# SwiGLU's upward products from the fifth block on as seven half-depth products, in a decoder trunk of fp32 weights split in two

## Chip, cores and metric

The kernel runs on one core of a Trainium2 chip. The metric is the device time of one execution in microseconds (us).

## The reference

One inference step of a trunk of two layers, on 512 columns of a prompt and 64 of eight samples. Each layer is an FFN, a mixer (retention, a Conformer convolution, a gated short convolution) and a second FFN; shift, scale and gate of each come from a conditioning vector by one more product ("modulation", `w_ada`).

```python
def swiglu(h, w1, w3, w2):
    return (jax.nn.silu(h @ w1) * (h @ w3)) @ w2
...
    ada = jax.nn.silu(c) @ w['w_ada'] + w['b_ada']
...
    h = modulate(rms_norm(x, w['g_ffn1']), sh1, sc1)
    x = x + 0.5 * gt1 * swiglu(h, w['w1_a'], w['w3_a'], w['w2_a'])
    h = modulate(rms_norm(x, w['g_mix']), sh2, sc2)
    mo, S_new, conf_new, sc_new = mixer(h, state_ret[l], state_conf[l], state_sconv[l], pos0, w)
    x = x + gt2 * mo
    h = modulate(rms_norm(x, w['g_ffn2']), sh3, sc3)
    x = x + 0.5 * gt3 * swiglu(h, w['w1_b'], w['w3_b'], w['w2_b'])
```

`h` has 1024 rows, w1 and w3 2816 columns each, w2 goes back to 1024. All is fp32.

## The kernel before

**Tiles.** Features lie on the partitions, the 576 columns in two halves of 288. A weight block of 128 outputs has 8 depth tiles of 128. Each fp32 number is split into a high part (a cast to fp32r) and a low part (the rest), and each product of 128x128 with 128x288 is three matmuls, hi.hi, hi.lo and lo.hi (`three`, L210 to L212). The hidden state `h` is held split in `hh` and `hl`.

**FFN.** Four FFNs run, called ffn0a, ffn0b, ffn1a and ffn1b here (layer, first or second). Each has 22 blocks f of w1 and w3. A block pair is one step: for each half, w1's and w3's product over all 8 depth tiles, then `post` (silu on ACT, L611; product on DVE, L612; split by ACT, L225, and DVE, L226). After the blocks of each entry of `GROUPS` come the 8 down products with w2 for these blocks. The last group's last four run in `end`, which lays the statistics of the next norm over its products: `stats` after one block of the first of them, `spread` (which needs a chain of small DVE operations, L317 to L343) after another of the second.

**Weights.** `pump` brings weights in along the list of keys of all steps. A 512 KB DMA on SP's queue fills one of RAW = 3 raw buffers (L142), ACT casts its high part (L161), DVE subtracts the low part (L121), and the raw buffer is free when DVE is done. Up to WB = 5 split weights are held. SP issues its DMAs in the order of the program, and an issue that must wait holds up those behind it.

**Modulation units.** While layer 0 runs, the modulation of everything later is computed in units (`ada_unit`): two tiles of 256 KB (L135) and four matmuls of 256 columns (L277). Two units stand behind nearly each block pair of ffn0a and ffn0b, one or two behind a down product. Up to ADA = 12 tiles are loaded ahead. Layer 1 has none.

**POOL** works in the mixers and in the norms, and adds the gated result of the sample columns to `xs` in the down products (L590).

## Time and profile before

| what | us |
| --- | --- |
| median of 3 runs | 3136.75 (3132.89 to 3136.88) |
| the profiled execution | 3134.75 |
| its span, first to last instruction | 3133.0 |
| TensorE busy in it | 3091.1 |

The profile is that of one execution; the span is what its rows cover, and 1.75 us lie around it. The mean granted TensorE clock was 0.996 of full speed (2.4 GHz).

### The profile page before, as it was taken

How to read it: one execution, taken by the hardware profiler on the slowest of the kernel's cores; microseconds unless marked ns; L12 is line 12 of the kernel's file. 1: busy time of each engine (PE TensorE's matmuls, PEld its weight loads, DVE VectorE, ACT ScalarE, POOL GpSimd, SP SyncE). 2: the span in 40 equal slices, each digit the busy share in tenths (PEclk: the TensorE clock that was granted, in tenths of full speed). 3: DMA queues.
4: the chain of work that ended last, by engine and by line, in shares of the span. 5: the costliest groups of instructions: out<-in, count | busy, mean ns of one | idle time of the engine just before them, and what ended most of it. 6: DMA issues, size and time to landing. Idle time of an engine off the chain costs nothing.

```text
span 3133.0 us, 55305 instructions
## 1 busy us (share of the span) xinstructions
PE 3091.1 (99%) x23412; PEld 2969.0 (95%) x23412; DVE 1535.0 (49%) x2840; ACT 873.4 (28%) x1468; POOL 405.7 (13%) x526
## 2 busy tenths in 40 slices
PE   7999999999999999999999999999999999999998
PEld 5999999899999999999999999988999999999998
DVE  5333336355995563323363333453669854533334
ACT  4222223222233342222232222332222333422221
POOL 1000004123113020000020000042221220200000
PEclk9999999999999999999999999999999999999999
DMA  7544423334322334636322222233352222222221
GB/s 277 167 155 149 148 94 125 100 85 116 89 77 80 115 122 147 207 129 214 113 82 75 88 88 81 88 117 112 84 120 84 81 95 95 78 85 81 81 83 56
DMA packets 142680, 349.67 MB, mean 112 GB/s; under 512 B 32400, under 2 KB 36752, under 8 KB 142432
## 3 DMA queue, kind: packets, MB, share of 16 engines
q1 hardware_dynamic: 135776, 329.35, 33.1%
q0 software_dynamic: 5504, 15.61, 1.9%
q8 instruction: 183, 3.00, 0.4%
q10 hardware_dynamic: 1152, 1.18, 0.1%
q14 instruction: 65, 0.53, 0.1%
HBM read 328.90 MB, written 12.45 MB: 109 GB/s over the span
## 4 chain that ended last, share of the span: by engine, by line
PE 92%; DVE 3%; POOL 1%; ACT 1%; DMA 1%; issue 1%; SPq 0%; ACTq 0%; DVEq 0%; POOLq 0%
PE pl L210 28%; PE pl L211 27%; PE pl L212 27%; PE pm L277 2%; PE pl L765 1%; PE pl L767 1%; PE pl L766 1%; PE pm L1164 1%; PE pm L1166 1%; DVE lo L121 1%; DMA ada<-in_ada 1%; DVE hl L383 1%; DVE t L393 0%; ACT hi L161 0%; DMA x<-in_x 0%
## 5 line engine op out<-in xcount | busy, mean ns | idle before, releaser
L211 PE MATMUL pl<-hl,hi 128*128 128x288 f32 x4576 | 1350.2, 295 | 11.0 <-POOL hl L421 9.6
L210 PE MATMUL pl<-hh,hi 128*128 128x288 f32 x4576 | 1360.3, 297 | 0.3 <-ACT hh L419 0.2
L212 PE MATMUL pl<-hh,lo 128*128 128x288 f32 x4576 | 1349.8, 295 | 0.0
L210 PEld LDWEIGHTS pl<-hh,hi 128*128 128x128 f32 x4576 | 860.2, 188 | 21.5 <-DVE t L612 10.7
L211 PEld LDWEIGHTS pl<-hl,hi 128*128 128x128 f32 x4576 | 860.2, 188 | 13.5 <-POOL hl L421 10.8
L212 PEld LDWEIGHTS pl<-hh,lo 128*128 128x128 f32 x4576 | 859.9, 188 | 0.0
L121 DVE TENSOR_TENSOR lo<-raw,hi 128x1024 fp32r<-128x1024 f32 (+1 forms) x446 | 551.8, 1239 | 520.0 <-ACT hi L161 519.7
L161 ACT CAST hi<-raw 128x1024 fp32r<-128x1024 f32 (+1 forms) x446 | 459.0, 1032 | 836.7 <-PE pl L211 635.6
L210 PE MATMUL pl<-ghi,hi 128*128 128x288 f32 x1408 | 419.9, 298 | 0.0
L212 PE MATMUL pl<-ghi,lo 128*128 128x288 f32 x1408 | 415.2, 295 | 0.0
L211 PE MATMUL pl<-glo,hi 128*128 128x288 f32 x1408 | 415.1, 295 | 0.0
L590 POOL TENSOR_TENSOR xs<-xs,t 128x64 f32<-128x64 f32 x112 | 41.1, 367 | 1833.8 <-DVE t L587 1833.6
L612 DVE TENSOR_TENSOR t<-t,pl 128x288 f32<-128x288 f32 x176 | 79.9, 454 | 404.1 <-PE pl L212 389.6
L210 PEld LDWEIGHTS pl<-ghi,hi 128*128 128x128 f32 x1408 | 264.4, 188 | 13.6 <-issue 11.5
L211 PEld LDWEIGHTS pl<-glo,hi 128*128 128x128 f32 x1408 | 264.5, 188 | 0.0
L212 PEld LDWEIGHTS pl<-ghi,lo 128*128 128x128 f32 x1408 | 264.4, 188 | 0.0
L210 PE MATMUL pl<-s,hi 128*128 128x288 f32 x768 | 227.8, 297 | 0.1
L211 PE MATMUL pl<-s,hi 128*128 128x288 f32 x768 | 226.6, 295 | 1.1 <-DVE s L226 1.1
L212 PE MATMUL pl<-s,lo 128*128 128x288 f32 x768 | 226.7, 295 | 0.0
L957 DVE SCALAR_TENSOR_TENSOR cv<-up,vec,cv 128x512 f32<-128x512 f32 x240 | 209.3, 872 | 5.4
L225 ACT CAST ghi<-t 128x288 fp32r<-128x288 f32 x176 | 76.1, 432 | 480.4 <-DVE t L612 480.4
L210 PEld LDWEIGHTS pl<-s,hi 128*128 128x128 f32 x768 | 144.3, 188 | 3.7 <-ACT t L867 2.1
(197 smaller groups left out, 2686.5 us busy)
## 6 DMA issues: line engine op xcount, KB each, us to landing
ada<-in_ada SPq DMA_DIRECT2D x288, 256.0 KB, 4.6
raw<-in_win SPq DMA_DIRECT2D x120, 512.0 KB, 3.6
raw<-in_w1a SPq DMA_DIRECT2D x44, 512.0 KB, 3.6
raw<-in_w3a SPq DMA_DIRECT2D x44, 512.0 KB, 3.6
raw<-in_w1b SPq DMA_DIRECT2D x44, 512.0 KB, 3.6
raw<-in_w3b SPq DMA_DIRECT2D x44, 512.0 KB, 3.6
raw<-in_w2a SPq DMA_DIRECT2D x32, 512.0 KB, 3.5
raw<-in_w2b SPq DMA_DIRECT2D x32, 512.0 KB, 3.5
```

The lines of the kernel that those rows point to most:

```text
L121: self.nc.vector.tensor_sub(lo, t, hi.bitcast(F32))
L161: nc.scalar.copy(hi[:, :m], t[:, c])
L210: mm(ps[:, :HB], hi[:, c], x[0][:, t], start=first, stop=False)
L211: mm(ps[:, :HB], hi[:, c], x[1][:, t], start=False, stop=False)
L212: mm(ps[:, :HB], lo[:, c], x[0][:, t], start=False, stop=last)
L225: nc.scalar.copy(hi, src)
L277: nc.tensor.matmul(self.ps_ada[32 * j:32 * j + 32, :], self.cs[:, k], w, start=(k == 0), stop=(k == 7))
L383: nc.vector.scalar_tensor_tensor(self.hl[:, k, c], t, s, hi.bitcast(F32), ALU.add, ALU.subtract)
L590: nc.gpsimd.tensor_add(xs, xs, t[:].rearrange("p b t -> p (b t)"))
L612: nc.vector.tensor_mul(s, s, ps[1][:, :HB])
L765: mm(ps, xh, wh, start=(k == 0), stop=False)
L957: nc.vector.scalar_tensor_tensor(cv[:, :S], up[:, k:k + S], w[:, k:k + 1], cv[:, :S], ALU.mult, ALU.add)
```

## The change

Blocks 0 to 3 of each FFN stay as they were, but block 3 runs its second half first. From block 4 on, two blocks f and f+1 ("a duo") are taken together, first w1 of both, then w3 of both. With the depth cut into a first and a second half of four tiles and the columns into halves, this is a 2x2 by 2x2 product of blocks, and `seven` computes it with seven products of half depth instead of eight: 7 x 4 x 3 matmuls on weights X, Y, Z (two tiles of 512 columns each, Y and Z made in place of the raws b and a) and S, which are sums of the raws' halves.

- `sums` makes these sums with four POOL additions of 128x512 and queues the casts as jobs. A pump in a seven does at most one job (`once`). A seven's casts are X, Y and Z of 1024 columns and S of 512, in place of two of 1024 for the two blocks.
- `forms` makes the matching sums of `h` (T2, T4, T5) in blocks 0 to 3; `last_forms` overwrites the second half of `hh` and `hl` in the middle of block 3. Until then `hold` keeps the first `sums` back.
- The results are put together behind the products: an ACT copy (s1), three DVE additions (u, v, u), and in `up1` and `up3` further ones; up3 multiplies three of its four results on POOL, and its splits run one post later.
- Two modulation units ("mids") stand inside each seven of ffn0a and ffn0b, between the third product and the fourth, as long as units are left, and one behind it. One stands behind each down product. Once the start is over only ADA_LATER = 4 tiles are loaded ahead, and pump takes their keys out of the list.
- `GROUPS` has four entries, the last with 6 blocks in place of 8; RAW goes from 3 to 4, SLOTS from 38 to 37, TEMPS from 12 to 10.
- The layernorm of the Conformer branch takes its mean with ones and a factor of -1/512 in the DVE operation, and the tile `one512` goes.

```diff
-GROUPS = ((0, 6), (6, 8), (14, 8))
+GROUPS = ((0, 6), (6, 6), (12, 4), (16, 6))
...
-RAW, WB, AHEAD, ADA = 3, 5, 4, 12
+RAW, WB, AHEAD, ADA, ADA_LATER = 4, 5, 4, 12, 4
...
-SLOTS, TEMPS = 38, 12
+SLOTS, TEMPS = 37, 10
...
-    def pump(self, later=False):
+    def load_ada(self, key):
+        self.split[key] = self.slot([128, 512], what="ada")
+        self.nc.sync.dma_start(self.split[key], self.source(key)[0])
+        self.whole += 1
+    def pump(self, later=False, cast=True):
         nc = self.nc
+        once = not cast
+        self.calls += 1
+        while self.gone and self.gone[0] <= self.calls:
+            self.gone.popleft()
+            self.whole -= 1
...
+            if self.quota > 8:
+                while self.n_dma < len(self.keys) and self.keys[self.n_dma][0] == "ada":
+                    self.adas.append(self.n_dma)
+                    self.n_dma += 1
+                if self.adas and self.whole < ADA_LATER and self.adas[0] <= self.cur + 2 * ADA:
+                    self.load_ada(self.keys[self.adas.popleft()])
+                    went = True
...
+            if self.jobs:
+                if not once and self.live + self.jobs[0][0] <= WB:
+                    self.jobs.popleft()[1]()
+                    if not later:
+                        self.rest()
+                    went = once = True
+            elif self.raw and self.quota and not (once and cast) and self.order[self.raw[0][0]] <= self.order[self.cur] + AHEAD:
                 key = self.keys[self.raw[0][0]]
                 spare = key in self.spare
-                if spare or self.live < WB:
+                if key in self.duo:
+                    if len(self.raw) > 1 and not self.hold:
+                        self.sums(key, self.raw.popleft()[1], self.raw.popleft()[1])
+                        went = True
...
+    def halves(self, key, t, n=1024):
+        w = [self.wp.tile([128, 1024], F32R, tag=x, bufs=WB, name=self.name(x)) for x in ("hi", "lo")]
+        self.live += 1
+        self.nc.scalar.copy(w[0][:, :n], t[:, :n])
+        self.late.append((w[1][:, :n], t[:, :n], w[0][:, :n]))
+        self.split[key] = w
...
+    def sums(self, key, a, b):
+        add = self.nc.gpsimd.tensor_add
+        s = self.wp.tile([128, 512], F32, tag="s1", bufs=1, name=self.name("s1"))
+        add(s, b[:, :512], b[:, 512:])
+        add(b[:, :512], b[:, :512], a[:, :512])
...
+        def z():
+            self.rest()
+            add(a[:, :512], a[:, :512], s)
+            add(a[:, 512:], a[:, 512:], a[:, :512])
+        def zh():
+            self.halves((*key, "Z"), a)
+            self.held -= 1
+        def yh():
+            self.halves((*key, "Y"), b)
+            self.held -= 1
+        self.jobs.extend(((1, lambda: self.halves((*key, "X"), a)), (0, z),
+                          (1, lambda: self.halves((*key, "S"), s, 512)), (1, yh), (1, zh)))
...
-            self.whole -= 1
+            if self.quota > 8:
+                self.gone.append(self.calls + 1)
+            else:
+                self.whole -= 1
...
+            nc.vector.tensor_sub(za[:, a], za[:, a], za[:, b])
+            nc.vector.tensor_sub(za[:, b], za[:, b], zb[:, b])
+            nc.vector.tensor_add(zb[:, b], zb[:, b], za[:, a])
+            nc.vector.tensor_sub(zb[:, a], zb[:, b], zb[:, a])
+            t5 = self.slot([128, NT], F32R, "t5")
...
+        self.T[7] = [(self.hh[:, i, HB:NT], self.hl[:, i, HB:]) for i in range(4)]
...
+    def last_forms(self):
+        for i, z in enumerate(self.zs):
+            hi, lo = self.T[7][i]
+            self.nc.scalar.copy(hi, z[:, HB:])
+            self.nc.vector.tensor_sub(lo, z[:, HB:], hi.bitcast(F32))
...
+        def product(ps, which, at, xs, first, last):
+            hi, lo = self.part(key, which)
+            for i, x in enumerate(xs):
+                c = slice(512 * at + 128 * i, 512 * at + 128 * i + 128)
+                k = dict(skip_group_check=True)
+                mm(ps, hi[:, c], x[0], start=first and i == 0, stop=False, **k)
+                mm(ps, hi[:, c], x[1], start=False, stop=False, **k)
+                mm(ps, lo[:, c], x[0], start=False, stop=last and i == 3, **k)
...
+        def more():
+            self.rest()
+            for fn in self.after:
+                fn()
+            self.after = []
+            self.pump(True)
+        p, q = bank(), bank()
+        product(p, "X", 0, quarter(0, 0), True, True)
+        s1 = self.temp([128, HB])
+        nc.scalar.copy(s1, p)
+        more()
+        product(q, "Y", 0, self.T[7], True, True)
+        u, v = self.temp([128, HB]), s1
+        nc.vector.tensor_add(u, s1, q)
+        more()
+        product(p, "X", 1, quarter(1, 0), False, True)
+        free("X")
+        post(0, 0, p)
+        more()
+        self.ada_done()
+        for m in mids:
+            self.ada_unit(*m)
+        product(q, "Z", 0, self.T[2], False, True)
+        nc.vector.tensor_sub(v, s1, q)
+        nc.vector.tensor_sub(u, u, q)
+        more()
+        r = bank()
+        product(r, "S", 0, self.T[5], True, True)
+        free("S")
+        post(1, 1, v, r)
+        more()
+        t = bank()
+        product(t, "Y", 1, self.T[4], True, True)
+        free("Y")
+        post(1, 0, v, t)
+        more()
+        product(r, "Z", 1, quarter(1, 1), False, True)
+        free("Z")
+        post(0, 1, u, r)
+        self.rest()
+        self.pump(True, False)
...
-            ps = self.run(w, xs, 1, 0, {0: 4, 1: 6}.get(i), {0: stats, 1: spread}.get(i))
+            ps = self.run(w, xs, 1, 0, {0: len(xs) // 2, 1: 3 * len(xs) // 4}.get(i), {0: stats, 1: spread}.get(i))
...
+            halves = (1, 0) if f == 3 else (0, 1)
...
+                if half > halves[1]:
+                    self.drain()
+                    self.last_forms()
+                    self.hold = False
+                    self.pump()
...
+            def up1(i, j, a, b=None):
+                t = self.temp([128, HB])
+                if b is None:
+                    nc.scalar.activation(t, a, AF.Silu)
+                else:
+                    if i == 0:
+                        nc.vector.tensor_add(t, a, b)
+                    else:
+                        nc.vector.scalar_tensor_tensor(t, a, -1.0, b, ALU.mult, ALU.subtract)
+                    nc.scalar.activation(t, t, AF.Silu)
+                acts[i, j] = t
+            def up3(i, j, a, b=None):
+                s = acts.pop((i, j))
+                if b is None:
+                    nc.vector.tensor_mul(s, s, a)
+                else:
+                    t = self.temp([128, HB])
+                    if i == 0:
+                        nc.vector.tensor_add(t, a, b)
+                    else:
+                        nc.vector.scalar_tensor_tensor(t, a, -1.0, b, ALU.mult, ALU.subtract)
+                    nc.gpsimd.tensor_mul(s, s, t)
+                c = slice(j * HB, (j + 1) * HB)
+                hi, lo = (x[:, c] for x in g[f + i])
+                def halves():
+                    nc.scalar.copy(hi, s)
+                    nc.vector.tensor_sub(lo, s, hi.bitcast(F32))
+                waiting.append(halves)
...
-                elif f > 1 or first:
-                    self.steps.append((pairs[f], lambda f=f: pair_step(pairs[f])))
-                    add_fill(0 if first and f == 5 else 2)
-            final = gi == 2
+                elif f > 3:
+                    for up in range(2 - f % 2 * 2):
+                        ks = [pairs[f][up], pairs[f + 1][up]]
+                        mids = [fill.popleft() for _ in range(min(2, len(fill)))]
+                        ks += [("ada", *u, i) for u in mids for i in range(2)]
+                        self.steps.append((ks, lambda f=f, up=up, mids=mids: duo_step(f, up, mids)))
+                        add_fill(2 if nfill > 72 else 1)
...
-                add_fill(2 if nfill > 60 else 1)
+                add_fill(1)
```

Three places show how instructions move. The first is SP's queue in ffn0b. Before, around blocks 12 and 13, the raws of one pair are followed by four modulation tiles (the word behind L142 or L135 is the tile; in brackets stands what the issue waits for, a DMA's completion or an engine):

```order
L142 DMA raw1752_12164<-in_w1b 128x1024 [waits DMAHW4_49,DVE_49]
L142 DMA raw1762_12242<-in_w3b 128x1024 [waits DMAHW5_49,DMAHW6_49,DVE_49,Activation_49]
L135 DMA ada1763_12244<-in_ada 128x512 [waits DMASW1_49,PE_49]
L135 DMA ada1764_12246<-in_ada 128x512 [waits DMAHW7_49,PE_49]
L135 DMA ada1765_12248<-in_ada 128x512 [waits DMAHW0_49,PE_49]
L135 DMA ada1766_12250<-in_ada 128x512 [waits DMAHW1_49,PE_49]
L142 DMA raw1794_12423<-in_w1b 128x1024 [waits DMAHW2_49,DVE_49]
L142 DMA raw1801_12489<-in_w3b 128x1024 [waits DMAHW4_49,DMAHW3_49,DVE_49]
```

After, at the last duos that have units, each seven queues the raws a and b of a later seven and then six tiles, or fewer. The tiles ada2660 and ada2661 are those of the second mid unit of the seven that follows, and raw2652 ahead of them waits for DVE's lo2651, the Z of that same seven, written at the turn to it; ada2690 and ada2691, for the second mid unit of the seven after, stand behind raw2678, which waits for lo2677, its Z:

```order
L167 DMA raw2647_16553<-in_w3b 128x1024 [waits DMAHW2_49,DVE_49]
L167 DMA raw2652_16575<-in_w3b 128x1024 [waits DMAHW3_49,DVE_49]
L136 DMA ada2660_16622<-in_ada 128x512 [waits DMAHW4_49,PE_49]
L136 DMA ada2661_16624<-in_ada 128x512 [waits DMAHW5_49,PE_49]
L136 DMA ada2665_16660<-in_ada 128x512 [waits DMAHW6_49,PE_49]
L136 DMA ada2666_16662<-in_ada 128x512 [waits DMAHW7_49,PE_49]
L136 DMA ada2667_16683<-in_ada 128x512 [waits DMAHW0_49,PE_49]
L136 DMA ada2668_16685<-in_ada 128x512 [waits DMAHW1_49,PE_49]
L167 DMA raw2673_16708<-in_w1b 128x1024 [waits DMAHW2_49,DVE_49,Activation_49]
L167 DMA raw2678_16732<-in_w1b 128x1024 [waits DVE_49,DMAHW3_49,Activation_49,Pool_49]
L136 DMA ada2690_16787<-in_ada 128x512 [waits DMAHW4_49,PE_49]
L136 DMA ada2691_16789<-in_ada 128x512 [waits DMAHW5_49,PE_49]
```

The loads have moved from up to six units ahead of their use to a place behind the second raw that is queued at the turn into the seven that uses them.

The second place is DVE at the end of the up3 seven of that duo and the start of the next up1 seven. L874 is the last addition after the seventh product (in pl2669), L883 a low part of a gated value, lo2672 and lo2677 are Y and Z of the next seven, lo2682 X of the one behind it; L577 belongs to the second product of the next seven:

```order
L132 TENSOR_TENSOR lo2672_16706<-raw2614_16386,hi2671_16705 128x1024
L874 TENSOR_TENSOR t2679_16746<-t2662_16638,pl2669_16687 128x288
L883 TENSOR_TENSOR glo2627_16445<-t2649_16568,ghi2626_16444 128x288
L132 TENSOR_TENSOR lo2677_16730<-raw2606_16341,hi2676_16729 128x1024
L132 TENSOR_TENSOR lo2682_16756<-raw2647_16553,hi2681_16755 128x1024
L883 TENSOR_TENSOR glo2625_16443<-t2653_16589,ghi2624_16442 128x288
L577 TENSOR_TENSOR t2692_16803<-t2689_16783,pl2688_16770 128x288
L355 COPY t2696_16830<-pm2638_16502 128x256
L587 TENSOR_TENSOR t2689_16783<-t2689_16783,pl2688_16770 128x288
L588 TENSOR_TENSOR t2692_16803<-t2692_16803,pl2688_16770 128x288
```

Before, DVE had here two low parts of weights, two multiplications and two low parts of gated values for a whole block pair; now Z's low part, for which SP's raw2678 waits, stands behind L874 and an L883.

The third place is POOL at the same duo. L220, L221, L225 and L226 are the sums for one seven, L877 the multiplications of up3 (in brackets the engine that each waits for):

```order
L220 TENSOR_TENSOR s12654_16593<-raw2614_16386 128x512 [waits DMAHW1_49,DVE_49]
L221 TENSOR_TENSOR raw2614_16386<-raw2614_16386,raw2606_16341 128x512 [waits DMAHW6_49,Pool_49]
L225 TENSOR_TENSOR raw2606_16341<-raw2606_16341,s12654_16593 128x512 [waits DVE_49,Pool_49]
L226 TENSOR_TENSOR raw2606_16341<-raw2606_16341 128x512 [waits Pool_49]
L877 TENSOR_TENSOR t2644_16547<-t2644_16547,t2670_16700 128x288 [waits DVE_49]
L877 TENSOR_TENSOR t2649_16568<-t2649_16568,t2675_16723 128x288 [waits DVE_49]
L877 TENSOR_TENSOR t2653_16589<-t2653_16589,t2679_16746 128x288 [waits DVE_49]
L220 TENSOR_TENSOR s12680_16752<-raw2652_16575 128x512 [waits DMAHW3_49,Activation_49]
L221 TENSOR_TENSOR raw2652_16575<-raw2652_16575,raw2647_16553 128x512 [waits DMAHW2_49,Pool_49]
```

Before, POOL had no instruction in the block pairs; now four sums precede the three multiplications, and the first sum behind them waits for raw2652.

## Rows read from the trace of the kernel before

**Rows 1.** Page of the profile: the span, the busy time of each engine (us, share, x instructions), and the shares of the chain that ended last, by engine.

```profile
span 3133.0 us, 55305 instructions
...
PE 3091.1 (99%) x23412; PEld 2969.0 (95%) x23412; DVE 1535.0 (49%) x2840; ACT 873.4 (28%) x1468; POOL 405.7 (13%) x526
...
PE 92%; DVE 3%; POOL 1%; ACT 1%; DMA 1%; issue 1%; SPq 0%; ACTq 0%; DVEq 0%; POOLq 0%
```

**Rows 2.** Timeline of TensorE in ffn0a, from the end of a product to the modulation units behind it: start us, duration us, line, operation, out<-in, shape, count.

```profile
399.82 0.29 PE L210 MATMUL pl<-hh,hi 128*128 128x288 f32 x1
...
405.21 0.29 PE L212 MATMUL pl<-hh,lo 128*128 128x288 f32 x1
405.43 1.07 PE L277 MATMUL pm<-ada,cs 128*32 128x256 f32 x16
406.43 0.40 PE L210 MATMUL pl<-hh,hi 128*128 128x288 f32 x1
```

**Rows 3.** What SP's DMA queue waited for: engine, line <- what released it: us in total, times, longest us.

```profile
SPq L142 <- DVE lo L121: 2112.9, 358, 15.4
SPq L135 <- PE pm L277: 189.5, 35, 12.6
```

**Rows 4.** What TensorE waited for, in the same form.

```profile
PE pm L350 <- DVE t L343: 3.7, 2, 3.0
PE pm L277 <- DMA ada<-in_ada: 1.3, 3, 0.8
```

**Rows 5.** Busy time in five stretches (start:end us): length, then busy us of each engine with its number of instructions, the granted clock (PEclk), the DMA share and GB/s; and behind them one row of the timeline, of the weight load that ends the idle time before the first stretch (in brackets the idle us and what ended it).

```profile
517.50:520.90 3.40, 3.40 (x16) 3.40 (x16) 3.01 (x7) 2.23 (x6) 3.40 (x5) 0.50 0.19 71
1166.00:1169.40 3.40, 3.40 (x16) 3.40 (x16) 2.67 (x7) 3.14 (x9) 1.33 (x2) 0.50 0.95 350
1637.00:1640.40 3.40, 3.31 (x25) 3.31 (x26) 2.69 (x7) 2.52 (x7) 1.55 (x3) 1.00 0.31 122
2710.00:2713.40 3.40, 3.14 (x24) 3.14 (x25) 2.67 (x7) 2.79 (x7) 1.30 (x3) 1.00 0.32 124
375.00:400.00 25.00, 25.00 (x205) 23.52 (x205) 8.90 (x14) 6.22 (x12) 0.00 (x0) 1.00 0.48 160
...
517.22 0.19 PEld L211 LDWEIGHTS pl<-hl,hi 128*128 128x128 f32 x1 [1.98 <-POOL hl L421]
```

**Rows 6.** DMA issues in three stretches of ffn0b (1285.3 to 1286.3, 1286.3 to 1286.6, 1285 to 1292 us), as line, queue, count, KB each, median us from issue to landing; and the landing times of the 16 modulation loads issued from 1240 to 1262 us.

```profile
raw<-in_w3b SPq DMA_DIRECT2D x1, 512.0 KB, 3.8
ada<-in_ada SPq DMA_DIRECT2D x1, 256.0 KB, 4.1
...
ada<-in_ada SPq DMA_DIRECT2D x1, 256.0 KB, 4.6
...
ada<-in_ada SPq DMA_DIRECT2D x4, 256.0 KB, 4.7
...
DMA to landing us min/median/max: 2.6/4.1/6.7
```

**Rows 7.** Groups of DVE instructions, shapes kept apart: line, operation, out<-in, shapes, count | busy us, mean ns of one | idle us before.

```profile
L121 DVE TENSOR_TENSOR lo<-raw,hi 128x1024 fp32r<-128x1024 f32 x414 | 520.5, 1259 | 494.7 <-ACT hi L161 494.5
...
L226 DVE TENSOR_TENSOR glo<-t,ghi 128x288 fp32r<-128x288 f32 x176 | 81.4, 462 | 87.7 <-ACT ghi L225 87.7
L612 DVE TENSOR_TENSOR t<-t,pl 128x288 f32<-128x288 f32 x176 | 79.9, 454 | 404.1 <-PE pl L212 389.6 <-ACT t L611 14.5
...
L121 DVE TENSOR_TENSOR w<-raw,w 128x512 fp32r<-128x512 f32 x20 | 12.5, 685 | 0.0
...
L326 DVE SCALAR_TENSOR_TENSOR t<-t,t 96x3 f32<-96x3 f32 x54 | 8.5, 157 | 1.8
```

**Rows 8.** Groups of ACT instructions, in the same form.

```profile
L161 ACT CAST hi<-raw 128x1024 fp32r<-128x1024 f32 x414 | 432.3, 1047 | 767.0 <-PE pl L211 595.9 <-PE pl L761 51.1 <-issue 34.3
L225 ACT CAST ghi<-t 128x288 fp32r<-128x288 f32 x176 | 76.1, 432 | 480.4 <-DVE t L612 480.4
L611 ACT ACTIVATE t<-pl 128x288 f32<-128x288 f32 x176 | 71.6, 407 | 168.8 <-PE pl L212 168.7
```

**Rows 9.** Groups of POOL instructions, in the same form.

```profile
L369 POOL TENSOR_TENSOR ssq<-ssq,t 128x288 f32<-128x288 f32 x18 | 14.5, 807 | 1.4
...
L411 POOL TENSOR_TENSOR s<-xs,t 128x512 f32<-128x512 f32 x5 | 9.0, 1806 | 23.1 <-ACT t L409 23.1
...
L415 POOL TENSOR_TENSOR s<-s,ada 128x512 f32<-128x512 f32 x5 | 6.4, 1277 | 0.4
L421 POOL TENSOR_TENSOR hl<-s,hh 128x512 fp32r<-128x512 f32 x5 | 6.3, 1260 | 0.0
L414 POOL TENSOR_TENSOR s<-s,ada 128x512 f32<-128x512 f32 x5 | 5.6, 1120 | 0.4
```

**Rows 10.** Timeline of DVE and POOL at the start of mixer 0: start us, duration us (of the whole group where a count is above 1), engine, line, operation.

```profile
508.29 2.35 DVE L121 TENSOR_TENSOR lo<-raw,hi 128x1024 fp32r<-128x1024 f32 x2
...
509.97 1.82 POOL L411 TENSOR_TENSOR s<-xs,t 128x512 f32<-128x512 f32 x1 [4.60 <-ACT t L409]
...
513.07 1.28 POOL L415 TENSOR_TENSOR s<-s,ada 128x512 f32<-128x512 f32 x1
...
513.33 2.10 DVE L121 TENSOR_TENSOR lo<-raw,hi 128x1024 fp32r<-128x1024 f32 x1
...
514.31 1.64 POOL L387 TENSOR_TENSOR hl<-t,hh 128x224 fp32r<-128x224 f32 x1
```

120 lines of the change are left out of this document (101 added, 19 removed).

## The prediction

> **What bounds the kernel now.** I read the page first. TensorE is busy 3091.1 of 3133.0 us and stands for 92% of the chain that ended last; DVE is at 49%, ACT at 28%, POOL at 13% [rows 1]. So time is won by taking matmuls out, as far as nothing else comes to end last. Next I took the price of a matmul from the timeline of TensorE in steady FFN work: 41 matmuls start between 399.82 and 405.21 us, 5.39 / 41 = 0.1315 us each [rows 2]. The two modulation units that follow take 1.07 us [rows 2], 0.53 each. Then I looked at what feeds it. SP's waits show a queue that works strictly in order: for 2112.9 us its head was a weight load waiting for a DVE low part to release a raw buffer, for 189.5 us a modulation load waiting for a tile [rows 3]. Today this costs TensorE almost nothing: it waited for a modulation tile 3 times, 1.3 us in all [rows 4], because up to 12 tiles, six units, are loaded ahead. Last, a stall can cost more than its length: the granted clock was 0.50, the level of 1.2 GHz, for 3.4 us behind two idle stretches of about 2 us, and stayed at 1.00 behind two others [rows 5].
>
> **The saving.** A block pair of w1 takes 2 blocks x 2 halves x 8 x 3 = 96 matmuls, a seven 7 x 4 x 3 = 84. There are 9 duos x 2 weights x 4 FFNs = 72 sevens, so 864 matmuls go: 864 x 0.1315 = **-113.6 us**, 28.4 in each FFN. A seven then lasts 11.05 us and a duo (w1 and w3) 22.1 instead of 25.3, or about 25.3 with the six modulation units in and behind its sevens in ffn0a and ffn0b. The operands keep their shapes, so I keep the price of one.
>
> **Modulation loads behind the raw buffers.** This is the largest loss that I find. For each seven SP now queues raw a, raw b and only then the tiles; raw b waits for the Z low part of the seven that is about to run, which DVE writes at the turn from one seven to the next (order of SP and DVE above). The second unit in the middle of this seven uses the first two tiles of that row. Let 0 be the end of the seventh product of the seven before it.
> - Need: the fill unit (0.53), three products of 12 (3 x 1.58 = 4.73) and the first mid unit (0.53) bring TensorE to the second unit at 5.8; its tiles are wanted at 5.8 and 6.1.
> - Arrival: a 512 KB raw landed 3.8 after its issue, and the two tiles queued behind it 4.1 and 4.6 after theirs, issued some 0.4 apart [rows 6]. So the tiles land 4.5 and 5.4 after raw b's issue. Single tiles of such a stretch took 2.6 to 6.7 [rows 6]; for the mean of many I let the second move between 4.6 (no longer than the raw's 3.8, issued 0.8 later) and 5.5 (the 4.7 of four tiles).
> - Issue of raw b behind an up1 seven (an up3 follows): after the seventh product DVE has the last addition of 0.45 and Z's low part of 1.26 to do [rows 7], 2.0 at least; with half of Y's low part still ahead of them I take 2.4. The second tile lands at 7.8: a stall of 1.7 (0.5 to 2.1).
> - Behind an up3 seven: Z's low part stands on DVE behind the low part of a gated value (L883), which waits for ACT's cast (0.43), and that for POOL's multiplication (0.81), queued behind the sums [rows 7 to 9]. Laid end to end I get 4.2; the second tile lands at 9.6: a stall of 3.5 (1.6 to 4.2).
> - The last up3 ahead of a group's down products has w2 loads and their low parts in the queue too, and the fill behind it is late as well: about 4 (2 to 5.5). The first seven of ffn0a and of ffn0b: 3 (1 to 4).
>
> By the order of these two FFNs there are 7, 7, 5 and 2 of these: 7 x 1.7 + 7 x 3.5 + 5 x 4 + 2 x 3 = **+62 us** (27 to 80), more than the 56.8 that the sevens save in them. A stall doesn't shorten the next one, since each counts from its own seventh product.
>
> **The clock behind these stalls.** 14 of them are near 3 us or longer. Half clock for 3.4 us let 16 matmuls through where 25 pass at full clock [rows 5]: 9 x 0.1315 = 1.2 us. It came behind 2 of the 4 idle stretches; I take 5 of 14, **+6** (0 to 17).
>
> **POOL and DVE in turn.** Before, POOL does nothing in 25 us of FFN [rows 5]; after, each duo has 8 sums of 128x512 and 3 multiplications. At 513 us the trace shows what that means: a DVE subtraction starts at 513.33 while POOL's L415 runs from 513.07 to 514.35, and takes 2.10 instead of 1.26, ending 1.08 after POOL did; POOL's next, started at 514.31, takes 1.64 [rows 10]. They take turns. So I add for a duo what both hold. DVE: 6 low parts at 1.08, and 2 of 512 elements (0.69) and 4 of 288 (0.46) less the same 0.18 each, 6.5 + 1.0 + 1.1 = 8.6. POOL: 8 x 1.26 + 3 x 0.81 = 12.5 [rows 7, 9]. The sum is 21.1 of 22.1 us: it just fits in ffn1a and ffn1b, with waits of a few tenths in the later up1 sevens. In ffn0 the duo has 25.3. **+5** (0 to 25). The price of a sum lies between L414's 1.12 and L411's 1.81, all of 128x512 [rows 9]. I take L421's 1.26, two full operands like a sum; L411 began at 509.97 while a low part ran to 510.64 [rows 10], so 0.67 of it is a turn that I count already.
> The Trainium skill, "SBUF — State Buffer", section "SBUF: two separate sides", says that the port pair of DVE and GpSimd is an exclusive lock held for the full instruction, whose loser fully blocks. The rows at 513 us agree on the blocking; on the length they give 1.08 of 1.26.
>
> **Smaller terms.** The first seven of an FFN waits for Y's low part: the sums are held back to the middle of block 3 and one job goes out at a time, so Y's cast stands behind that block's post (0.41 + 0.45 + 0.43 + 0.46) and takes 1.05 + 1.26 itself [rows 7, 8], 4.1 after the block's end, against 1.6 of cover by the first product, or 2.6 where two units stand between in ffn0. That is 2.5 and 1.5 at most and nothing if casts run beside the post; I take 1.7 twice and 0.6 twice, **+4.6** (0 to 8). The last group is 6 blocks instead of 8, so 21 instead of 30 matmuls (2.8 instead of 3.9 us) lie over the chain of small DVE operations up to L343, for which TensorE waited 3.7 us in two places [rows 4]; some twenty of 0.157 [rows 7] make 3.2: about 1 in each FFN, **+4** (0 to 8). Added casts, the forms and a fourth group's eight down rows lie on engines at half load; the slot and the two temps fewer I cost at nothing, up to 3 if an allocation of a mixer waits. The layernorm's edit puts one DVE operation for one.
>
> **The sum.** 3134.75 - 113.6 + 62 + 6 + 5 + 4.6 + 4 = 3102.8 for the profiled execution. That lay 2.0 below the median of the runs shown (3136.75), so on their scale it is some 3104.8; I say **3104**.
>
> **Rivals.**
> - *The tiles come in time*: no 62, no 6: 3136.75 - 113.6 + 13.6 = 3037. For it: the smallest landing of 2.6. Against: with a landing of 5.4, raw b must be issued by 0.7, and one low part alone takes 1.26 after the product.
> - *Turns as long as whole instructions*: DVE 6 x 1.26 + 2 x 0.69 + 4 x 0.46 = 10.8, with POOL 23.3 in place of 22.1 in 18 duos of ffn1, 22 us instead of 5: 3122. For it: POOL's 1.64 beside its neighbour; against: the 1.08. By the page of the Trainium skill named above this is the one to expect.
> - *The loads at their slow bound*, each long stall with half clock behind it: 80 + 17 instead of 68: 3134, no change. For it: the landings up to 6.7.
> - *The other side: POOL ends last in ffn1.* If a sum takes L411's 1.81 whatever DVE does, a duo holds 8 x 1.81 + 2.4 + 8.6 = 25.5: 18 x (25.5 - 22.1) = 61 instead of 5, while in ffn0 units and stalls cover it: 3161, slower. It decides once it eats the remaining 32 us, from 24.2 a duo on, a sum of 1.65. For it: the sums fall where DVE is busiest; against: L414, L415 and L421 at 1.12 to 1.28 [rows 9].
>
> **How the numbers follow.** The sum's own case has 0.60 (3070 to 3125 by the bounds of the loads), tiles in time 0.12, whole lengths 0.08, slow loads 0.10, POOL as the bound 0.10. A measurement here tells 0.2%, 6.3 us: faster is below 3130.5, slower above 3143. Faster takes 0.60 + 0.12 + 0.08, less 0.03 for the first case's tail: 0.77. Same is that tail and half of the slow loads, 0.08. Slower is the other half and POOL, 0.15. The range 3050 to 3155 leaves out the tiles in time and half of POOL's case, 0.17.
>
> **What would show it.** Right: TensorE waits at the mid units for DMA of modulation tiles, some 20 to 35 times in ffn0a and ffn0b and 40 to 80 us in all; in ffn1 a duo lasts 22 to 23 us; SP's head waits for Z's low part; POOL is busy some 12.5 to 15 us a duo. Wrong: the later duos of ffn0b no longer than those of ffn1b but for 3.2 us of units, or a duo of ffn1 above 24 us with TensorE waiting for DVE or POOL, or matmuls of a seven that start other than 0.13 apart.

## The result: 37 us slower, and the profile after

The changed kernel takes 3174.06 us (3170.86 to 3181.51, 4 runs) against 3136.82 before: a ratio of 1.0125, 95% interval 1.0106 to 1.0145. The forecast was 3104, 3050 to 3155, and slower had been given a chance of 0.15.

The page of the profile after, in the lines of [rows 1]:

```profile
span 3169.1 us, 55762 instructions
...
PE 3042.8 (96%) x22548; PEld 2871.2 (91%) x22548; DVE 2026.4 (64%) x3561; ACT 1038.6 (33%) x1761; POOL 989.0 (31%) x969
...
PE 76%; DVE 11%; DMA 5%; issue 3%; ACT 3%; POOL 2%; SPq 0%; ACTq 0%; DVEq 0%; POOLq 0%
```

TensorE is busy 48 us less and idle 84 us more, and stands for 76% of the chain instead of 92%. DMA stands there with 5% (4% of it the modulation tiles), DVE with 11%.

The four FFNs, before and then after: each stretch runs from the statistics of the norm ahead of it to those at its end. The columns are length, busy time of TensorE, of its weight loads, DVE, ACT and POOL with their instructions, the granted clock, the DMA share and GB/s:

```profile
26.50:488.60 462.10, 460.08 (x3629) 427.24 (x3629) 173.73 (x296) 120.61 (x203) 19.60 (x35) 0.99 0.46 155
1152.80:1608.40 455.60, 453.83 (x3669) 426.81 (x3670) 161.26 (x284) 114.70 (x190) 17.05 (x29) 1.00 0.47 157
1624.00:2033.20 409.20, 407.39 (x3075) 407.10 (x3076) 157.49 (x258) 113.39 (x189) 16.45 (x29) 1.00 0.27 84
2697.20:3106.40 409.20, 407.39 (x3075) 407.14 (x3076) 153.34 (x253) 111.75 (x185) 16.23 (x29) 1.00 0.25 77
```

```profile
26.00:506.10 480.10, 452.98 (x3433) 405.07 (x3433) 294.86 (x477) 161.70 (x277) 166.62 (x146) 0.98 0.45 150
1169.80:1658.60 488.80, 457.26 (x3475) 404.75 (x3475) 288.28 (x464) 155.71 (x263) 161.51 (x140) 0.98 0.44 146
1674.20:2077.00 402.80, 390.08 (x2880) 386.32 (x2880) 280.86 (x440) 155.15 (x264) 162.48 (x140) 0.99 0.28 87
2742.00:3145.00 403.00, 389.83 (x2881) 385.47 (x2881) 276.79 (x435) 153.64 (x260) 163.35 (x140) 0.99 0.26 78
```

ffn0a is 18.0 us longer, ffn0b 33.2, ffn1a and ffn1b 6.4 and 6.2 shorter, where the sevens alone should have taken some 25 us out of each of these stretches (195 matmuls fewer in ffn1a, at 0.13 us). POOL's busy time rises from 17 to some 160 us.

What TensorE waited for after (us in total, times, longest; compare [rows 4]):

```profile
PE pm L350 <- DMA ada<-in_ada: 39.6, 39, 3.2
PE pm L409 <- DVE ssq L442: 15.9, 9, 4.4
PE pl L285 <- ACT t L793: 11.4, 10, 1.7
PE pl L557 <- DVE t L577: 10.6, 13, 0.8
...
PE pl L559 <- DVE lo L132: 6.5, 7, 1.4
...
PE pl L557 <- ACT hi L210: 6.3, 5, 2.1
```

For a ledger that closes I laid the starts of all matmuls in the two traces end to end. An interval belongs to the matmul that ends it. For weights, what is above 0.1317 us (the mean of an undisturbed product, in blocks as in sevens) is put into a class by its size and by the granted clock:

| class | before | after | change |
| --- | --- | --- | --- |
| matmuls of weights at 0.1317 each (20736, 19872) | 2730.9 | 2617.1 | -113.8 |
| modulation matmuls, whole intervals | 78.8 | 143.7 | +64.9 |
| 0.45 us and more, in the sevens | 0 | 30.5 | +30.5 |
| 0.45 us and more, in all other products | 16.8 | 30.1 | +13.3 |
| excess at half clock | 3.2 | 18.6 | +15.4 |
| 0.17 to 0.45 us, mostly the two matmuls behind a break of the row | 34.0 | 43.9 | +9.9 |
| the norms' statistics | 36.0 | 47.6 | +11.6 |
| all else | 217.3 | 222.2 | +4.9 |
| first to last start (rows are rounded) | 3117.1 | 3153.6 | +36.5 |

### The profile page after: what moved, and what is told of

Same layout as the page of the kernel before. It is cut to its first block, busy times and chain, and to the rows that moved or that the text cites. A ratio compares the mean times of both kernels' runs of the same rounds, so it can differ in the third digit from the quotient of the medians.

```text
span 3169.1 us, 55762 instructions
## 1 busy us (share of the span) xinstructions
PE 3042.8 (96%) x22548; PEld 2871.2 (91%) x22548; DVE 2026.4 (64%) x3561; ACT 1038.6 (33%) x1761; POOL 989.0 (31%) x969
## 4 chain that ended last, share of the span: by engine, by line
PE 76%; DVE 11%; DMA 5%; issue 3%; ACT 3%; POOL 2%; SPq 0%; ACTq 0%; DVEq 0%; POOLq 0%
PE pl L285 17%; PE pl L286 16%; PE pl L287 16%; PE pl L557 6%; PE pl L559 6%; PE pl L558 6%; DMA ada<-in_ada 4%; DVE lo L132 4%; PE pm L350 2%; PE pl L1037 1%; DVE glo L883 1%; PE pl L1039 1%; PE pl L1038 1%; PE pm L1436 1%; POOL t L877 1%
## 5 line engine op out<-in xcount | busy, mean ns | idle before, releaser
L132 DVE TENSOR_TENSOR lo<-raw,hi 128x1024 fp32r<-128x1024 f32 (+2 forms) x553 | 739.5, 1342 | 242.0 <-ACT hi L196 213.3
L285 PE MATMUL pl<-hh,hi 128*128 128x288 f32 x2320 | 692.0, 298 | 11.7 <-ACT t L793 11.4
L286 PE MATMUL pl<-hl,hi 128*128 128x288 f32 x2320 | 685.5, 295 | 9.1 <-POOL hl L494 6.4
L287 PE MATMUL pl<-hh,lo 128*128 128x288 f32 x2320 | 684.2, 295 | 1.5 <-DVE lo L132 1.5
L196 ACT CAST hi<-raw 128x1024 fp32r<-128x1024 f32 (+2 forms) x337 | 316.1, 945 | 557.5 <-PE pl L286 345.6
L285 PEld LDWEIGHTS pl<-hh,hi 128*128 128x128 f32 x2320 | 436.2, 188 | 20.6 <-ACT t L793 13.7
L286 PEld LDWEIGHTS pl<-hl,hi 128*128 128x128 f32 x2320 | 436.2, 188 | 12.2 <-POOL hl L494 7.7
L287 PEld LDWEIGHTS pl<-hh,lo 128*128 128x128 f32 x2320 | 436.1, 188 | 1.9 <-DVE lo L132 1.9
L557 PE MATMUL pl<-hh,hi 128*128 128x288 f32 x1152 | 345.6, 300 | 6.3 <-ACT hi L210 6.3
L559 PE MATMUL pl<-hh,lo 128*128 128x288 f32 x1152 | 343.5, 298 | 6.5 <-DVE lo L132 6.5
L558 PE MATMUL pl<-hl,hi 128*128 128x288 f32 x1152 | 342.4, 297 | 0.0
L210 ACT CAST hi<-raw 128x1024 fp32r<-128x1024 f32 x216 | 225.2, 1044 | 249.3 <-PE pl L286 176.5
L772 POOL TENSOR_TENSOR xs<-xs,t 128x64 f32<-128x64 f32 x144 | 66.1, 460 | 567.7 <-DVE t L769 567.4
L557 PEld LDWEIGHTS pl<-hh,hi 128*128 128x128 f32 x1152 | 218.9, 190 | 18.5 <-issue 10.7
```

The costliest lines, as they stand in the source:

```text
L132: self.nc.vector.tensor_sub(lo, t, hi.bitcast(F32))
L196: nc.scalar.copy(hi[:, :m], t[:, c])
L210: self.nc.scalar.copy(w[0][:, :n], t[:, :n])
L285: mm(ps[:, :HB], hi[:, c], x[0][:, t], start=first, stop=False)
L286: mm(ps[:, :HB], hi[:, c], x[1][:, t], start=False, stop=False)
L287: mm(ps[:, :HB], lo[:, c], x[0][:, t], start=False, stop=last)
```

## The experiments

Each edit is of the changed kernel. "Ledger" is the table above, made for the run's own trace in the same way.

**Tiles ahead.**

```diff
-RAW, WB, AHEAD, ADA, ADA_LATER = 4, 5, 4, 12, 4
+RAW, WB, AHEAD, ADA, ADA_LATER = 4, 5, 4, 12, 6
```

> One number of the changed kernel is altered: 6 modulation tiles (three units) may be loaded ahead instead of 4. In the changed kernel the time between the starts of modulation matmuls (each to the one before) is 143.7 us against 78.8 before, 65 more. Theory (tiles queue behind raw b on SP): the two tiles of the second unit in a seven are now issued ahead of raw a and raw b, TensorE's waits for modulation tiles fall from 39.6 us to under 12, the 143.7 falls to 80 to 95, and some half clock goes with it: 3174 to 3105 to 3125. Rival (a unit inside a seven costs more by itself, whenever its tiles land): the 143.7 stays above 125, time above 3155. Rival (no slot is free for two more tiles, so that the tile's issue waits for a slot on SP and the raws behind it come late): waits of TensorE move to low parts of weights, time not below 3160.

Measured: 3123.92 us (3122.22 to 3130.01), 0.9962 of before (0.9949 to 0.9974). The modulation's entry falls from 143.7 to 84.0. What TensorE still waited for in this run:

```profile
PE pl L557 <- DVE t L577: 16.3, 18, 1.1
...
PE pm L350 <- DMA ada<-in_ada: 9.5, 5, 7.6
```

Of the 9.5 us for tiles, 7.6 are one wait at the start. So of the 64.9 us that the modulation had gained, 59.7 were late tiles, and the place of the units inside a seven can have cost 5.2 at most in this entry (the breaks of the row have one of their own). In their place the waits for L577 rose from 10.6 to 16.3 us: up1 sevens of ffn0 that had been covered by the tiles now wait for DVE as those of ffn1 do.

**Units spread.** The second unit goes from ahead of the fourth product to behind the fifth:

```diff
-        for m in mids:
+        for m in mids[:1]:
             self.ada_unit(*m)
         product(q, "Z", 0, self.T[2], False, True)
...
         post(1, 1, v, r)
         more()
+        for m in mids[1:]:
+            self.ada_unit(*m)
```

> The changed kernel with the second of the two units inside a seven moved from the place ahead of the fourth product to behind the fifth; tiles ahead stay 4. Theory (the second unit's tiles land 8.8 to 9.7 us after the seven's start, behind raw b): wanted some 3.2 us later, most of them are there, the 143.7 us fall to 85 to 105, time 3120 to 3140. Rival (units inside a seven cost by themselves, two places instead of one break TensorE's row more often): 143.7 stays or rises, 3170 to 3185.

Measured: 3129.58 us (3127.01 to 3134.9), 0.998 of before. The modulation's entry is 98.9, as expected. One more break of the row in each of 26 sevens raised the class of 0.17 to 0.45 us in the sevens from 15.7 to 23.6, 0.3 us for a break.

**The pending casts one product later.**

```diff
+        def more(late=True):
             self.rest()
-            for fn in self.after:
-                fn()
-            self.after = []
+            if late:
+                for fn in self.after:
+                    fn()
+                self.after = []
             self.pump(True)
...
         nc.scalar.copy(s1, p)
-        more()
+        more(False)
```

> The changed kernel with the pending casts and low parts of the gated values (L882, L883) that a seven runs behind its first product run behind its second instead, after the addition u (L577). In the changed kernel twelve of the up1 sevens in ffn1a and ffn1b take 12.2 us instead of 11.1, and TensorE waits there for L577 ahead of the fourth product. Theory (DVE stands in order behind L883, which waits its turn behind a POOL sum): the twelve take 11.1 to 11.3, 13 us less in ffn1 and some 3 in ffn0: 3174 to 3157 to 3162. Rival (the turns of POOL and DVE together bound the duo, 21 of 22 us): the wait only moves to another low part, time within 5 us of 3174.

Measured: 3166.12 us (3163.95 to 3169.28), 8 less than the changed kernel, where 12 to 17 were expected. The up1 sevens of 12.2 us in ffn1, of which there are ten and not twelve, went to 11.4 us, and the wait for L577 is gone from the list, but in ffn0 some of it was lost again (modulation 148.8). The order on DVE was the cause in ffn1.

**The forms' casts, and the seven's first casts ahead of the overwritten h.**

```diff
+            yield
             nc.scalar.copy(hi, zb)
             nc.scalar.copy(t5[:, a], za[:, a])
             yield
...
             self.T[4].append((hi[:, a], lo[:, a]))
-            yield
...
-            hooks = {k: more for k in (2, 5)}
+            hooks = {k: more for k in (1, 3, 5)}
...
-                    self.last_forms()
                     self.hold = False
                     self.pump()
+                    self.last_forms()
```

> The changed kernel with two things altered around blocks 0 to 3: each round of forms puts its ACT casts one step behind its DVE sums (and there are three hooks instead of two in each of the first products to make up for it), and the first weight casts of the sevens are queued ahead of the overwriting of the second half of h. In the changed kernel TensorE waits 11.4 us in ten places for a silu of blocks 1 to 3 that stands on ACT behind such a cast, and the first sevens of the four FFNs take 5 to 10 us more than the next ones, partly at half clock. Theory (both come from the forms' order on ACT and DVE): the waits for the silu nearly vanish and each first seven loses 2 to 4 us less: 3174 to 3145 to 3158. Rival (the first sevens are late for the sums on POOL and the one job at a time, not for the forms): only the 10 us for the silu go, 3162 to 3166.

Measured: 3167.92 us (3163.62 to 3172.59). The waits for the silu fell from 11.4 to 7.0 us, yet the first sevens of ffn1 became longer, 19.0 and 17.8 us: their second product waited 3.1 us for Y's high cast. That stood on ACT behind block 3's own post, and this on DVE behind the four low parts of the overwritten h, which took 3.74 us beside the sums instead of 1.55. The time is above both cases: two edits in one run pulled against each other. A later run takes the first alone.

**The sums held back less.**

```diff
             halves = (1, 0) if f == 3 else (0, 1)
+            if f == 3:
+                self.hold = False
```

> The changed kernel with one line moved: the sums and casts of the first seven are no longer held back until the second half of h is overwritten in the middle of block 3, but until block 3 begins, 6.3 us earlier. In the changed kernel the first sevens of the four FFNs have 10 us of waits (X's cast, Y's and X's low parts) and 13 us of half clock. Theory (these are late because their casts are queued behind the four casts of the overwritten h and behind block 3's own post): first sevens of ffn1a and ffn1b go from 16.4 and 17.2 to 11 to 13 us, those of ffn0a and ffn0b lose 3 to 5 us, time 3174 to 3150 to 3160. Rival (what is late there is the overwritten h, which stays where it is): the first product comes in time, but the second waits as long for h, 3168 to 3176. Rival (casts of the seven now stand ahead of block 3's post on ACT and DVE, and TensorE waits in block 3 instead): same time.

Measured: 3175.14 us (3172.72 to 3186.85), no gain; my theory failed here. The time is that of the third case, and casts of the seven do stand ahead of block 3's post, but TensorE waits in the first sevens and not in block 3. In ffn1b, with the seven already begun (2810.55):

```profile
2816.12 4.51 DVE L132 TENSOR_TENSOR lo<-raw,hi 128x1024 fp32r<-128x1024 f32 x2
...
2816.95 0.40 ACT L793 ACTIVATE t<-pl 128x288 f32<-128x288 f32 x1
...
2820.56 0.44 DVE L794 TENSOR_TENSOR t<-t,pl 128x288 f32<-128x288 f32 x1
```

The second product waits 3.83 us for Y's cast, which now stands on ACT behind the overwriting of h. Then DVE does the low parts of Y and Z (4.51 us for two, beside a sum), and block 3's own product on DVE, L794, comes 3.2 us after its silu. TensorE waits another 1.5 us for ACT's copy (L573) behind it. The first sevens of ffn1 take 21.9 and 22.3 us.

**Groups of 6, 4, 4 and 8 blocks.**

```diff
-GROUPS = ((0, 6), (6, 6), (12, 4), (16, 6))
+GROUPS = ((0, 6), (6, 4), (10, 4), (14, 8))
```

> The changed kernel with groups of 6, 4, 4 and 8 blocks instead of 6, 6, 4 and 6; all else the same, matmuls too. In the changed kernel TensorE waits in front of the norms' statistics for the sums of squares 11.6 us in eight places after the start, against 3.1 before: 2.96 in front of the second half's and 0.9 of the first half's at the end of an FFN. Theory (the last four down products of an FFN have 18 matmuls instead of 24 a half, 3.2 us less over a chain of DVE work of fixed length): these waits go back to 3 to 4 us, 3174 to 3163 to 3167. Rival (DVE's chain is longer than before, whatever lies over it): waits stay near 11, 3172 to 3176. Rival (eight blocks of split gated values leave the modulation tiles no slot in ffn0b): tiles wait longer there and the time is 3174 or more.

Measured: 3159.94 us (3158.7 to 3161.92), 14 less. The statistics' waits, of 15.9 us in nine places after (4.4 of them at the start):

```profile
PE pm L409 <- DVE ssq L442: 7.4, 7, 4.6
```

In the ledger the statistics return to 36.1, the value before (36.0).

**Tiles ahead and pending casts together** (the first and third edit).

> Two edits together: 6 tiles ahead (alone 3123.9, 50 less) and the gated values' pending casts behind the second product (alone 3166.1, 8 less). With 6 tiles ahead alone, the up1 sevens of ffn0a and ffn0b, which had been covered by the wait for tiles, wait 1.1 to 1.5 us for L577 as well. Theory (both are separate terms, and the second is now worth something in ffn0 too): up1 sevens at 11.4 in ffn1 and 12.5 to 12.9 in ffn0, 3123.9 less 8 less 7, 3107 to 3112. Rival (once the tiles are in time, POOL and DVE in turn bound the sevens of ffn0 too): the wait moves elsewhere, 3115 to 3124.

Measured: 3107.85 us (3106.49 to 3110.14), 0.9909 of before (0.9894 to 0.9924). Together they take 66 us away, 8 more than the sum of the two alone (50 and 8), as expected: modulation 84.7, and no product of a seven waits 0.45 us any more but in the first of each FFN.

**No sums.**

```diff
-        add = self.nc.gpsimd.tensor_add
-        s = self.wp.tile([128, 512], F32, tag="s1", bufs=1, name=self.name("s1"))
-        add(s, b[:, :512], b[:, 512:])
-        add(b[:, :512], b[:, :512], a[:, :512])
+        s = b[:, 512:]
...
             self.rest()
-            add(a[:, :512], a[:, :512], s)
-            add(a[:, 512:], a[:, 512:], a[:, :512])
```

> The changed kernel without its sums: the four POOL additions of each seven are left out and X, Y, Z and S are cast from the raws as they lie, so the weights of the sevens are others; casts, low parts, products and loads stay. Theory (DVE's low parts take turns with POOL's sums: they take 1.34 us on the mean against 1.26 before, and L577 is late behind them): low parts at 1.2 to 1.26, the up1 sevens of ffn1 at 11.1 to 11.4, first sevens 1 to 3 us shorter, waits for modulation tiles 5 to 15 us less since Z's low part comes earlier; 3174 to 3140 to 3157. Rival (the waits come from the order on DVE and SP alone, not from turns): L577 waits as before, within 6 us of 3174.

Measured: 3146.72 us (3143.11 to 3152.69), 27 less. DVE's low parts of 1024 elements, in the changed kernel and then without sums (busy us, mean ns of one):

```profile
L132 DVE TENSOR_TENSOR lo<-raw,hi 128x1024 fp32r<-128x1024 f32 x425 | 611.9, 1444 | 226.7 <-ACT hi L196 199.7 <-ACT hi L210 21.8 <-PE pm L1421 4.3
```

```profile
L132 DVE TENSOR_TENSOR lo<-raw,hi 128x1024 fp32r<-128x1024 f32 x425 | 555.0, 1311 | 224.6 <-ACT hi L196 198.2 <-ACT hi L210 22.1 <-PE pm L1416 4.3
```

The mean falls from 1444 to 1311 ns, the up1 sevens of ffn1 take 11.13 us, and the wait for L577 is gone. The waits for tiles and for the silu in this run (lines stand 5 lower):

```profile
PE pm L345 <- DMA ada<-in_ada: 49.9, 36, 8.3
...
PE pl L280 <- ACT t L788: 6.2, 6, 1.6
```

The wait for the silu halves (11.4 to 6.2). That for tiles doesn't fall: 8.3 of the 49.9 us are one wait at the start, and the modulation's entry in the ledger is 144.7. So the sums cost some 27 us, and nothing of that through the tiles. By the ledger it lies in the sevens (30.5 to 14.3, most of it the wait for L577), in the blocks and down products (30.1 to 23.7) and in smaller entries. The run takes away the turns with DVE and the sums' own length together, and doesn't part the two; POOL's multiplications and their turns stay in it, and the mean of 1311 is still above the 1259 of [rows 7].

**The forms' edit alone** (the first three pieces of the diff of the fourth run).

> The changed kernel with the forms' edit alone (each round's ACT casts one step behind its DVE sums, three hooks instead of two); the overwriting of the second half of h stands ahead of the seven's first casts again, as in the changed kernel. With both edits the waits for the silu fell from 11.4 to 7.0 us, but the second product of each first seven then waited 1.4 to 3.4 us for the overwritten h, whose low parts took turns with the sums (3.73 us for four instead of 1.55). Theory (the forms' chain on ACT and DVE makes the first sevens late, the turns did the rest): first sevens of ffn1a and ffn1b at 13 to 15.5 us instead of 16.4 and 17.2, silu waits 5 to 8 us, time 3154 to 3163. Rival (X's cast behind the overwriting is what the first product waits for, whatever the forms do): the first product waits 2 us as before, 3164 to 3172.

Measured: 3162.17 us (3156.47 to 3167.03), 12 less, with 16.1 us of waits in the first sevens down to 8.8:

```profile
PE pl L285 <- ACT t L793: 7.0, 6, 1.5
...
PE pl L557 <- ACT hi L210: 1.6, 2, 0.8
```

**Four edits together**: 6 tiles, pending casts later, groups of 6, 4, 4, 8, the forms' edit.

> Four edits together: 6 tiles ahead (alone 50 us), pending casts behind the second product (8 alone, 66 with the first), groups of 6, 4, 4 and 8 (14 alone), and the forms' casts one step later (5 to 15 expected alone). If the terms are separate, 3107.9 - 14 - 5 to 10: 3082 to 3090, and the waits left are the first sevens', some 6 to 8 us in blocks 1 to 3 and the half clock behind them. Rival (eight blocks of split gated values and six tiles don't fit the slots together, so that tiles or raws come late in ffn0b): 3095 to 3110, with waits for modulation tiles above 12 us.

Measured: 3079.35 us (3077.48 to 3081.61), 0.9821 of before (0.9806 to 0.9835): faster than both kernels, and a little below the 3082 to 3090 expected. What is left:

```profile
PE pm L409 <- DVE ssq L442: 7.5, 7, 4.7
...
PE pl L285 <- ACT t L794: 7.0, 6, 1.5
PE pl L557 <- ACT hi L210: 6.3, 4, 2.4
PE pl L559 <- DVE lo L132: 6.3, 6, 1.4
```

**The order in the middle of block 3**, on top of these four:

```diff
-                    self.last_forms()
                     self.hold = False
-                    self.pump()
+                    self.pump(True)
+                    self.last_forms()
+                    self.rest()
```

> The four edits of 3079.35 us, and in the middle of block 3 the order X's high cast, overwriting of h, X's low part (instead of overwriting, X's high cast, X's low part), so that ACT casts X 1.4 us earlier while DVE still subtracts for h before POOL gets its turn. Theory (the first product of a first seven waits for X behind the four casts of h): the first sevens' waits of 15.0 us and half clock of 7.8 become 8 to 12 and 3 to 7, time 3070 to 3077. Rival (their waits are Y's low parts, one job later in either order): within 3 us of 3079. Rival (the second product then waits for the overwritten h, as it did where that stood last): 3080 to 3086.

Measured: 3082.02 us (3081.38 to 3083.65), so by its time the first rival: within 3 us. Its reason holds only in part. The first sevens' waits are 16.7 us instead of 15.0: in ffn0 that for X's high cast falls from 2.6 us to 1.3, and that for X's low part, now behind the low parts of h, rises from 0.9 to 2.7. Three attempts at this place have moved the wait and not removed it.

## Why the prediction was wrong, step by step

**The saving was right**: the row of matmuls keeps 0.13 us in the sevens, and a duo of ffn1 lasts 22.3 us where it doesn't wait and 11.1 + 12.2 = 23.3 where its up1 seven waits for L577 (ten of 18), near the 22 to 23 named. The first duo of each FFN is the exception, with 27.6 and 28.3 us in ffn1.

**The tiles were right, in place and size**: 62 forecast, 64.9 measured, and one number (4 to 6) took 59.7 of it away. By the four groups of the forecast's sum, as the length of the modulation's intervals above that of the run with six tiles, it is 14.3 us in the up3 sevens (11.9 forecast), 19.2 in the up1 sevens behind them (24.5), 19.2 at the group ends (20) and 7.2 in the first sevens (6), so one group was put too high and one too low, and the sum is closer than its parts. In ffn0b SP issued two raws (here of w2) and then six tiles, and TensorE stood at the second unit (SP's rows, then DVE's and POOL's, then TensorE's; in brackets the wait):

```profile
1375.63 2.90 SPq L167 DMA_DIRECT2D raw<-in_w2b  x2
1378.62 3.75 SPq L136 DMA_DIRECT2D ada<-in_ada  x6
```

```profile
1376.01 0.96 POOL L877 TENSOR_TENSOR t<-t,t 128x288 f32<-128x288 f32 x1 [1.52 <-DVE t L874]
...
1376.22 4.05 DVE L132 TENSOR_TENSOR lo<-raw,hi 128x1024 fp32r<-128x1024 f32 x2
```

```profile
1379.95 0.64 PE L350 MATMUL pm<-ada,cs 128*32 128x256 f32 x8
1383.70 1.74 PE L350 MATMUL pm<-ada,cs 128*32 128x256 f32 x8 [3.11 <-DMA ada<-in_ada]
```

The forecast counted from the end of the seventh product before, behind which the fill unit starts at 1374.41. The second raw, in the place of raw b, was issued at 1378.20, 3.8 us after that (4.2 forecast), and the tiles landed after 9.3 and 9.9 us (8.7 and 9.6 forecast). Behind the up1 sevens the second raw came at 2.1 instead of 2.4. One reason of the step was wrong in part: POOL's sums don't make Z's low part late, since without them the second raw came only 0.1 us earlier in the same seven and the waits stayed. POOL's multiplication does: Z's low part, the first of the two in DVE's row, takes 1.83 us beside L877, and 1.82 in the run without sums.

**The step that failed is that of the smaller terms**, "lie on engines at half load", together with the turns and the clock: 6 + 5 + 4.6 + 4 = 19.6 us in the sum, 85.6 in the ledger (all but the first two rows). By parts, of which the second overlaps with the others and is not to be added to them:

- *First sevens*, 4.6 (0 to 8) forecast: 16.1 us of waits, and 8.1 of half clock in them. I priced Y's low part alone, at 2.5 for a seven at most. In ffn1b also X was late, behind the four casts of the overwritten h on ACT, and Y and Z stood on DVE beside the sums:

```profile
2797.74 1.43 ACT L541 CAST hh<-za 128x288 fp32r<-128x288 f32 x4
...
2799.07 1.04 ACT L210 CAST hi<-raw 128x1024 fp32r<-128x1024 f32 x1
...
2800.14 1.22 DVE L132 TENSOR_TENSOR lo<-raw,hi 128x1024 fp32r<-128x1024 f32 x1 [0.34 <-ACT hi L210]
...
2800.16 0.40 PE L557 MATMUL pl<-hh,hi 128*128 128x288 f32 x1 [2.11 <-ACT hi L210]
...
2803.20 1.38 POOL L226 TENSOR_TENSOR raw<-raw 128x512 f32<-128x512 f32 x1
...
2803.78 4.10 DVE L132 TENSOR_TENSOR lo<-raw,hi 128x1024 fp32r<-128x1024 f32 x2 [0.34 <-ACT hi L210]
...
2805.71 0.61 PE L559 MATMUL pl<-hh,lo 128*128 128x288 f32 x1 [1.05 <-DVE lo L132]
```

TensorE began the seven at 2800.16 after 2.1 us of idle time, waited again for X's low part, and for Y's until 2805.71: two low parts took 4.10 us, since POOL's L226 held the first up for 0.8 and the sum after it (2804.53 to 2806.79) the second for 1.1. The clock was at its lower level for the 10.2 us from 2800.50 on (35 matmuls where some 77 fit):

```profile
2800.50:2810.70 10.20, 8.45 (x35) 7.89 (x34) 8.10 (x8) 4.10 (x7) 7.76 (x5) 0.50 0.27 79
```

- *Turns*, 5 (0 to 25) forecast: 27 by the run without sums, 2.2 of it waits of the first sevens and with the sums' own length in it. The sum over a duo was no bad guide, since it does fit in 23.3 us; but half of the price came from one place in the order. In ffn1a:

```profile
1822.49 1.82 DVE L132 TENSOR_TENSOR lo<-raw,hi 128x1024 fp32r<-128x1024 f32 x1
...
1823.19 2.27 POOL L220 TENSOR_TENSOR s<-raw 128x512 f32<-128x512 f32 x1
...
1824.24 1.54 DVE L883 TENSOR_TENSOR glo<-t,ghi 128x288 fp32r<-128x288 f32 x1
...
1825.70 0.44 DVE L577 TENSOR_TENSOR t<-t,pl 128x288 f32<-128x288 f32 x1
```

POOL's sum waits for the low part of X and then runs to 1825.46; the low part of a gated value (L883), started at 1824.24, waits for that; and the addition u (L577) that TensorE needs ahead of its fourth product stands behind it. This is the 1.1 us of each such seven, some 14 us in 13 sevens, ten of them in ffn1. The sums, at their shortest 1.26 to 1.29 us, took longer on the mean than the 1.26 that I took, since DVE holds them up as well:

```profile
L221 POOL TENSOR_TENSOR raw<-raw,raw 128x512 f32<-128x512 f32 x72 | 128.0, 1777 | 5.6
L220 POOL TENSOR_TENSOR s<-raw 128x512 f32<-128x512 f32 x72 | 116.7, 1621 | 70.2 <-DVE lo L132 58.8 <-DMA raw<-in_w1a 11.4
...
L226 POOL TENSOR_TENSOR raw<-raw 128x512 f32<-128x512 f32 x72 | 98.5, 1368 | 5.6
L225 POOL TENSOR_TENSOR raw<-raw,s 128x512 f32<-128x512 f32 x72 | 96.2, 1336 | 242.8 <-DVE lo L132 164.5 <-issue 65.0 <-DVE t L870 11.7
```

The Trainium skill, "SBUF — State Buffer", section "SBUF: two separate sides", has the later of the two fully blocked for the whole instruction; here POOL's L220 ended 1.15 us after DVE's low part, near the whole 1.27 that it takes at its shortest.

- *Forms*, nothing forecast: 13.3 us of waits in the blocks and down products, 11.4 of them for a silu of blocks 1 to 3 that stood on ACT behind a cast which waited for five DVE sums. In ffn1b's first round DVE's sums are held up by POOL, by the forms' own additions (L510) and then by the first seven's first two sums. `hold` keeps those back in the order of ACT and DVE only: POOL had nothing ahead of them that waits and ran them 33 us before the seven, where I had counted all of the sums from the middle of block 3 on.

```profile
2760.81 6.54 POOL L510 TENSOR_TENSOR za<-hh,hl 128x576 f32<-128x576 f32 x4
2767.31 1.50 POOL L220 TENSOR_TENSOR s<-raw 128x512 f32<-128x512 f32 x1
...
2769.16 1.43 DVE L523 TENSOR_TENSOR zb<-zb 128x288 f32<-128x288 f32 x1
...
2770.62 0.68 ACT L526 CAST thi<-zb 128x576 fp32r<-128x576 f32 x1 [9.27 <-DVE zb L523]
```

DVE's last sum takes 1.43 us here, and 0.46 in the run without sums (2751.23 there), where this round's wait is gone and all silu waits together fall to 6.2 us. But POOL isn't the whole of it: in the next round POOL is idle, DVE's last sum takes 0.46 us, and TensorE still waits 1.50 (2781.05). ACT is busy a third of the span; what counted was the place in its queue. The forms' edit took four of the ten waits away (4.4 us); the other six stayed.

- *The end of an FFN*, 4 (0 to 8) forecast: 11.6. I priced nine matmuls between `stats` and `spread`. The whole of the last four down products is shorter by 24 matmuls in the second half, 3.2 us, over DVE work that stays, and TensorE waits 2.67 us in front of the second statistics at three ends. Groups with eight blocks at the end took it all back.
- *The clock*, 6 (0 to 17) forecast: 15.4, with 8.1 in the first sevens, where I had expected no long stall, and less behind the tiles.
- *Breaks of the row*, nothing forecast: 9.9. Already [rows 2] show the first matmul behind two units at 0.40 us instead of 0.29, and in that trace the next one starts 0.24 us after it; in ffn0 a duo has four such breaks, before it had two.

None of the rivals was the outcome: the other side that I named, POOL ending last in ffn1, didn't happen (ffn1 is faster), though its 3161 lies nearest to the time. Several small waits did, each of which had been priced alone, or put at nothing, against an average load. With the tiles in time the kernel is at 3123.9, where by my sum it would have been at 3037: that is the size of the error in the terms other than the tiles.

**What stays open** is the wait of the first seven in each FFN. The forms' edit alone halves it (16.1 to 8.8), but with six tiles ahead 15.0 are left, 10 of them in ffn0; three orders around the overwritten h gave nothing.

## What to carry to other kernels

A change that takes an eighth of some products off the bound engine and hands additions, casts and loads to the others is to be priced by each queue's order, not by its load: ask at every place where TensorE needs a result what stands ahead of it on DVE, ACT, POOL and SP, and what those wait for. Two units of loads ahead are few when they queue behind a buffer that is released by another engine; a third took 50 us away. Where work of fixed length is hidden at the end of a loop, count what the last group leaves to hide it.
